# Moving an overflow branch from the front of a mixture-of-experts loop to its end

## The chip, the cores and the metric

The kernel runs on one core of one Trainium2 chip. The metric is the device time of one execution in microseconds (us). The engines that the text names are TensorE (PE, with its weight loads PEld), VectorE (DVE), ScalarE (ACT), GpSimd (POOL) and SyncE (SP), which issues most DMAs. Each engine has its own queue of instructions and goes through it in order. Semaphores make one engine wait for another.

## What is computed

Two layers over 512 positions of width 1024. In each layer a token mixer and a cross-attention to 256 memory positions are projected, added and normalised. Then comes a mixture of 16 experts with two experts for each position:

```python
def grouped_moe(x, router_w, router_b, w_gate, w_up, w_down):
    ...
    combine = jnp.einsum('tk,tke->te', gate,
                         jax.nn.one_hot(idx, N_EXPERTS, dtype=jnp.float32)).astype(x.dtype)
    out = jnp.zeros_like(xt)
    for e in range(N_EXPERTS):
        h = jax.nn.silu(xt @ w_gate[e]) * (xt @ w_up[e])
        out = out + combine[:, e:e + 1] * (h @ w_down[e])
    return out.reshape(bsz, seq, d)
...
    f = grouped_moe(x, router_w, router_b, w_gate[i], w_up[i], w_down[i])
    x = layer_norm(ALPHA * x + f, ln2_g[i], ln2_b[i])
```

The kernel computes each expert for the positions that chose it, up to 128 of them. If an expert was chosen by more, the rest are its overflow. With these inputs no expert overflows.

## The kernel before

*Products.* Every float32 operand is split into a high and a low part, and `mm3` (line 200) makes one product of three matmuls: high by high, high by low and low by high. ACT makes the high part (line 168 for weights, line 207 for activations), DVE the low one (lines 169 and 208).

*Pages and weights.* SBUF is dealt out as 24 pages of equal size, `page` and `drop`, first freed first used. The stream `W` fetches the weights, 1 MB each, by SP (line 147) into a free page, and `pump` fetches and splits as far as pages allow: it leaves `W.keep` pages free, has at most `W.flight` loads in flight and goes down to `W.stop` loads that wait. In the experts the split parts go to a ring of pages of their own (`W.rings(8)`).

*Routing.* `mixer_end` (line 1042) writes the normalised rows to DRAM, into `x1d` (what the experts read) and into `rd` (to which they add), makes the router's tables, and `overflow` (line 599) counts the positions of each expert: `nover` is the number of overflowing blocks, written by DVE at line 610 in the last of four small operations behind the matmuls of line 603.

*Experts.* `experts` (line 651) runs once per layer. POOL gathers the rows of an expert from `x1d` (line 668), PE transposes them (line 677), ACT and DVE split them into `xgt`. Gate and up products follow (`gate_up`, tiles ga and ua), then silu and product h (lines 696, 693), transposes of h (line 702), the down product (tile ya), and POOL scatters the result with addition into `rd` (line 664). The loop is a software pipeline: the down product of expert e-1 comes behind the gate and up products of expert e. PE, ACT and DVE are in an order written by hand (`manual_schedule`) for experts 0 to 14; expert 15 and all else are placed by a scheduler, which may queue an instruction earlier than the text has it when its operands are there. `tc.issue_after(ins)` ties instructions behind `ins` on its engine.

*The branch.* `more` (line 891) reads `nover` into a register of every engine (line 893) and branches (line 894). Behind the branch stands a loop over 48 possible blocks, of which nothing runs here. Its body uses `x1d`, `rd`, `y1` and, before the change, two halves of the page `hy`. In the version before it stands ahead of the first expert's transposes. In the first layer `fill` computes keys and values of the next layer (tile va) just ahead of it; in the second, `fill` does nothing and eight filler matmuls (`keep_warm`, line 299, operands of ones) stand there instead.

*The end of a layer.* For the last expert the scatter is replaced: rows of `rd` are loaded as x (SP, line 768), the layer norm's rows by POOL (line 293), and matmuls add x and the last expert's result (lines 785 to 787). The work for that is again in an order by hand and begins with eight filler matmuls that are tied behind the last up product, `up`.

Of the kernel before, what the change touches and what calls it, by code (L numbers as in the profile page):

```python
# [27 lines left out]
P = 128  # L28
D = 1024
KB = D // P  # L30
# [7 lines left out]
FE = 512  # L38
# [9 lines left out]
def trunk(ctx, tc, x, mem, w_in_a, sgu_ln_g, sgu_ln_b, sgu_w, sgu_b, w_in_b, conv_w, w_kv, w_out,  # L48
# [15 lines left out]
    def page(name, shape, dtype=FT, of=None):  # L64
        of = free_pages if of is None else of
        assert of, f"no page for {name}; held: {sorted(v[1] for v in held.values())}"
        i = of.pop(0)
        uid[0] += 1
        t = pages.tile(shape, dtype, name=f"{name}_{uid[0]}", tag=f"pg{i}", bufs=1)
        held[id(t)] = (i, name, t)  # L70
        return t

    def drop(*ts):
        for t in ts:
            i, name, _ = held.pop(id(t))
            W.home(name).append(i)

    def acc(name="acc"):
        return psum.tile([P, 512], FT, name=name, tag="A", bufs=4)

    def bank(shape, name="bank"):
        return psum.tile(shape, FT, name=name, tag="B", bufs=3)
# [115 lines left out]
    W = Stream()  # L198

    def mm3(o, a, b, start, stop):  # L200

        pe.matmul(o, a[0], b[0], start=start, stop=False)  # L202
        pe.matmul(o, a[0], b[1], start=False, stop=False)  # L203
        return pe.matmul(o, a[1], b[0], start=False, stop=stop)  # L204

    def split_to(hi, lo, src):
        r = act.activation(hi, src, AF.Copy)  # L207
        vec.tensor_tensor(lo, src, hi, op=OP.subtract)  # L208
        return r
# [85 lines left out]
    def keep_warm(n):  # L295

        t = bank([P, 4, P], "warm")
        for _ in range(n):
            pe.matmul(t, ones_b, ones_b[:, None, :].to_broadcast([P, 4, P]), start=True, stop=True)
# [12 lines left out]
    memh = page("memh", [P, KB, NMEM], FR)  # L312
    meml = page("meml", [P, KB, NMEM], FR)
# [5 lines left out]
    def keys_values(after=None):  # L319
        kt = page("kt", [P, 2, H, NMEM], FR)  # L320
        vt = page("vt", [P, 2, 2, MW], FR)
        a = [acc("ka") for _ in range(H)]
        for j in range(4):
            g = W.next()
            for kk in range(2):
                k = 2 * j + kk
                for h in range(H):
                    cs = slice(h * P, (h + 1) * P)
                    mm3(a[h][:, :NMEM], (g[:, 0, kk, cs], g[:, 1, kk, cs]), (memh[:, k, :], meml[:, k, :]),
                        k == 0, k == KB - 1)  # L330
            W.done(g)
        for h in range(H):
            split_to(kt[:, 0, h, :], kt[:, 1, h, :], a[h][:, :NMEM])
        a = [acc("va") for _ in range(2)]
        for j in range(4):
            g = W.next()
            for kk in range(2):
                k = 2 * j + kk
                for m in range(2):
                    ms = slice(m * P, (m + 1) * P)  # L340
                    with ExitStack() if after is None or j < 3 else tc.issue_after(after):
                        mm3(a[m], (memh[:, k, ms], meml[:, k, ms]), (g[:, 0, kk, :], g[:, 1, kk, :]),
                            k == 0, k == KB - 1)
            W.done(g)
        for m in range(2):
            split_to(vt[:, 0, m, :], vt[:, 1, m, :], a[m])
        return kt, vt

    def x_transposed():
        xh = [page("xh", [P, 4, S], FR) for _ in range(2)]  # L350
# [300 lines left out]
    def experts(i, lnp, fill, after, stop, fine=False):  # L651
# [4 lines left out]
        hy = page("h", [P, 4, FE])  # L656
# [15 lines left out]
        def xtrans(e):  # L672
            for q in range(2):
                t = bank([P, 4, P], "xt")
                for k in range(4):
                    k0 = 4 * P * q + 2 * P * (k // 2) + k % 2
                    pe.transpose(t[:, k, :], xg[:, e % 2, k0:k0 + 2 * P - 1:2], ident)  # L677
                split_to(xt[:, 0, 4 * q:4 * q + 4, :], xt[:, 1, 4 * q:4 * q + 4, :], t)
# [38 lines left out]
        def scaled(e):  # L717
            return lambda n, o: act.activation(ys[e % 2][:, n * 512:(n + 1) * 512], o, AF.Copy, scale=tabs[e][1])  # L718
# [3 lines left out]
        if i:  # L722
            with tc.issue_after(last_entry[-1]):
                keep_warm(8)
        fill()
        more(i, hy)
        W.keep, W.flight = 0, 4
        W.ahead, W.whole, W.on_pool = 6, True, lambda n: False
        W.rings(8)
        xtrans(0)  # L730
        gather(2)
        W.pump()
        order = ExitStack()
# [1 line left out]
        for e in range(E):  # L735
            if e == last:
                order.close()
            up = gate_up(e, (lambda: (down(last - 1, scaled(last - 1)), scatter(last - 1))) if e == last else None)
            if e + 1 < E:
                xtrans(e + 1)  # L740
            if e + 3 < E:
                gather(e + 3)
            if e == 5:
                W.parts += 2
            if 0 < e < last:
                down(e - 1, scaled(e - 1))
                scatter(e - 1)
            if e == last - 3:
                W.keep = 4
                W.stop = stop - 2 if stop else 0  # L750
            if e == last:
                W.rings(0)
                drop(xt, xg)
                selp = page("selt", [P, 2, NC, P], FT)
                for c in range(NC):
                    vec.tensor_scalar(selp[:, 0, c, :], slot1, posp[:, c, last:last + 1], None, op0=OP.is_equal)
                t = bank([P, NC, P], "selt")
                for c in range(NC):
                    pe.transpose(t[:, c, :], selp[:, 0, c, :], ident)
                selt = page("selr", [P, NC, P], FR)  # L760
                vec.tensor_copy(selt, t)
                drop(selp)
                xs[:] = [page("x", [P, 2, D]) for _ in range(2)]
                xrow[:] = [xs[c // 2][:, c % 2, :] for c in range(NC)]
                with tc.issue_after(added[last - 1].ins):
                    lnp = ln_params(*lnp, pool_e)
                for c in range(NC):
                    W.behind = sp.dma_start(xrow[c], rd[i][c * P:(c + 1) * P, :]).ins
            if e < last:
                htrans(e)  # L770
# [60 lines left out]
        def half_moments(c):  # L831
            part(c, 0)
            part(c, 1)
            moments(c)

        with tc.manual_schedule(engines={ET.PE, ET.Activation, ET.DVE, ET.Pool}):
            with tc.issue_after(up.ins):
                keep_warm(8)
            htrans(last)
            keep_warm(4)  # L840
            down(last, parts)
            act.activation(lnp[:, 0], lnp[:, 0], AF.Copy, scale=ALPHA)
            if fine:
                for c in range(3):
                    total(c)
                half_moments(0)
                part(1, 0)
                finish(0, "pool")
                after(0)
                part(1, 1)  # L850
                total(3)
                moments(1)
                centred(1)
                finish(1, "both")
                after(1)
                half_moments(2)
                centred(2)
                finish(2, "split")
                after(2)
                half_moments(3)  # L860
                centred(3)
                finish(3, "vec")
                after(3)
            else:
                total(0)
                total(1)
                half_moments(0)
                centred(0)
                finish(0, "dve")
                total(2)  # L870
                half_moments(1)
                centred(1)
                finish(1, "dve")
                after(0)
                total(3)
                W.after = after(1).ins
                half_moments(2)
                if "both" != "pool":
                    centred(2)
                finish(2, "both")  # L880
                half_moments(3)
                if "split" != "pool":
                    centred(3)
                finish(3, "split")
# [95 lines left out]
    W.after = last_mem.ins  # L980
    W.pump()
    W.after = None
    kt, vt = keys_values()
    xh, xl = x_transposed()
    for c in range(NC):
        transposed(xrow[c], KB, lambda q: xh[q], lambda q: xl[q], c * P)
# [16 lines left out]
    a = project_t(xh, xl)  # L1003
# [6 lines left out]
    a = project(xh, xl)  # L1010
# [5 lines left out]
    a = project_t(xh, xl)  # L1016
# [52 lines left out]
    kv1 = []  # L1069
# [4 lines left out]
    def fill0():  # L1074
        W.on_pool = lambda n: False
        kv1.append(keys_values(last_entry[-1]))
        drop(memh, meml)
    xhl = []

    def next_x(c):  # L1080
# [2 lines left out]
        xh, xl = xhl[0]  # L1083
        return transposed(xrow[c], KB, lambda q: xh[q], lambda q: xl[q], c * P)
    experts(0, (ln2_g[0], ln2_b[0]), fill0, next_x, stop)
    kt, vt = kv1[0]
    xh, xl = xhl[0]


# [1 line left out]
    a = project_halves(xh, xl)  # L1091
# [7 lines left out]
    a = project_t(xh, xl)  # L1099
    for h in range(H):  # L1100
        act.activation(cgp[:, h, :], a[h], AF.Copy)
    a = project_t(xh, xl)
# [7 lines left out]
    a = project_t(xh, xl)  # L1110
# [48 lines left out]
```

## Time and profile before

| | us |
|---|---|
| median of 3 timed runs | 1035.75 |
| lowest and highest of them | 1032.32, 1035.86 |
| the profiled execution | 1031.97 |
| its span, first to last instruction | 1030.1 |

The profile is of one execution. Of each instruction it has start and duration, of each idle stretch of an engine what ended it, of each window the granted TensorE clock (1.00 is 2.4 GHz, 0.50 is 1.2 GHz). The experts of the first layer run from about 213 to 510 us, those of the second from about 706 to 1007 us. "Idle before" in a timeline is the wait of the engine just ahead of a row, with what ended it.

### The profile page before, as it was taken

What the parts mean: (1) busy time and instruction counts of PE and PEld (TensorE: products, weight loads), DVE (VectorE), ACT (ScalarE), POOL (GpSimd) and SP (SyncE); (2) the same over time, 40 slices, a digit from 0 to 9 for tenths busy, and PEclk for the clock granted to TensorE, in tenths of its full rate; (3) what the DMA queues carried; (4) which work ended last, traced back from release to release, by engine and by line L of the source; (5) the groups of instructions that cost most, each with busy time, mean ns of one, the idle gap of its engine ahead of it and who ended that gap; (6) DMA issues with size and microseconds to landing.
All of it is one profiled execution on the core that took longest, in us unless ns stands there. A gap on an engine that the chain in (4) does not pass through costs nothing. (4 is left out here: it accounts for less than half of the span.)

```text
span 1030.1 us, 12721 instructions
## 1 busy us (share of the span) xinstructions
PE 983.7 (95%) x4815; PEld 810.6 (79%) x4816; DVE 774.2 (75%) x884; ACT 627.7 (61%) x684; POOL 200.5 (19%) x111
## 2 busy tenths in 40 slices
PE   8999999969999999999999999977899999999995
PEld 6788888858888888888679887865688888888873
DVE  4738567867989898898894455675689898988975
ACT  4626532556788787878643414233687887878763
POOL 0000002112332413321110000221133324233023
PEclk9999999989999999999999999987899999999998
DMA  9813266667999999999880425490799999999944
GB/s 321 294 42 123 91 237 247 244 225 265 364 367 333 366 360 360 360 357 362 282 320 1 164 82 207 131 396 25 232 330 362 372 327 383 359 362 355 357 87 160
DMA packets 102219, 273.30 MB, mean 265 GB/s; under 512 B 10442, under 2 KB 10966, under 8 KB 102152
## 3 DMA queue, kind: packets, MB, share of 16 engines
q1 hardware_dynamic: 89480, 242.84, 64.5%
q0 software_dynamic: 11808, 26.97, 9.4%
q10 hardware_dynamic: 864, 2.62, 0.7%
q8 instruction: 39, 0.64, 0.2%
q14 instruction: 28, 0.23, 0.1%
HBM read 262.22 MB, written 26.21 MB: 280 GB/s over the span
## 5 line engine op out<-in xcount | busy, mean ns | idle before, releaser
L169 DVE TENSOR_TENSOR low<-raw,high 128x2048 fp32r<-128x2048 f32 x189 | 427.9, 2288 | 80.9 <-ACT high L168 79.4
L168 ACT ACTIVATE high<-raw 128x2048 fp32r<-128x2048 f32 x189 | 355.1, 1910 | 22.7 <-PE ga L204 10.1
L668 POOL DMA_INDIRECT xg<-x1d,idxs x32 | 83.2, 2601 | 299.6 <-PE xt L677 270.5
L168 ACT ACTIVATE split<-raw 128x1024 fp32r<-128x1024 f32 x66 | 68.9, 1058 | 71.1 <-PE za L204 26.0
L202 PE MATMUL ya<-high,ht 128*128 128x512 f32 x256 | 103.8, 406 | 0.0
L169 DVE TENSOR_TENSOR split<-raw,split 128x1024 fp32r<-128x1024 f32 x61 | 73.6, 1221 | 39.6 <-ACT split L168 38.9
L204 PE MATMUL ga<-high,xgt 128*128 128x512 f32 x248 | 99.1, 399 | 2.9 <-DVE xgt L208 2.9
L204 PE MATMUL ya<-high,ht 128*128 128x512 f32 x256 | 101.3, 396 | 0.1
L203 PE MATMUL ya<-low,ht 128*128 128x512 f32 x256 | 101.1, 395 | 0.0
L202 PE MATMUL ga<-high,xgt 128*128 128x512 f32 x248 | 100.7, 406 | 0.1
L203 PE MATMUL ga<-low,xgt 128*128 128x512 f32 x248 | 98.4, 397 | 0.0
L204 PE MATMUL ua<-high,xgt 128*128 128x512 f32 x248 | 97.1, 392 | 0.0
L202 PE MATMUL ua<-high,xgt 128*128 128x512 f32 x248 | 96.9, 391 | 0.0
L203 PE MATMUL ua<-low,xgt 128*128 128x512 f32 x248 | 96.8, 390 | 0.0
L169 POOL TENSOR_TENSOR split<-raw,split 128x1024 fp32r<-128x1024 f32 x5 | 11.9, 2383 | 267.0 <-DVE sto L475 147.0
L202 PE MATMUL za<-xh,split 128*128 128x512 f32 x160 | 61.6, 391 | 2.0 <-ACT xh L207 2.0
L203 PE MATMUL za<-xl,split 128*128 128x512 f32 x160 | 62.5, 391 | 0.0
L204 PE MATMUL za<-xh,split 128*128 128x512 f32 x160 | 61.5, 389 | 0.0
L204 PEld LDWEIGHTS ga<-high,xgt 128*128 128x128 f32 x248 | 47.4, 191 | 14.1 <-DVE xgt L208 4.0
L204 PEld LDWEIGHTS ya<-high,ht 128*128 128x128 f32 x256 | 48.1, 188 | 12.8 <-DVE ht L208 1.3
L664 POOL DMA_INDIRECT rd<-h,idxs x16 | 40.4, 2523 | 89.3 <-ACT h L718 79.6
L202 PEld LDWEIGHTS ya<-high,ht 128*128 128x128 f32 x256 | 48.4, 189 | 10.5 <-ACT ht L207 0.6
(250 smaller groups left out, 1886.2 us busy)
## 6 DMA issues: line engine op xcount, KB each, us to landing
raw<-in_w_gate_dram SPq DMA_DIRECT2D x64, 1024.0 KB, 9.8
raw<-in_w_up_dram SPq DMA_DIRECT2D x64, 1024.0 KB, 9.6
raw<-in_w_down_dram SPq DMA_DIRECT2D x64, 1024.0 KB, 10.5
raw<-in_w_kv_dram SPq DMA_DIRECT2D x8, 1024.0 KB, 7.4
raw<-in_w_out_dram SPq DMA_DIRECT2D x8, 1024.0 KB, 8.0
raw<-in_w_in_b_dram SPq DMA_DIRECT2D x8, 1024.0 KB, 11.1
raw<-in_w_in_a_dram SPq DMA_DIRECT2D x6, 1024.0 KB, 5.4
x1d<-x POOLq DMA_DIRECT2D x8, 512.0 KB, 6.0
```

What stands on the lines that cost most here:

```text
L168: act.activation(high, src, AF.Copy)
L169: (pool_e if self.on_pool(self.count) else vec).tensor_tensor(low, src, high, op=OP.subtract)
L202: pe.matmul(o, a[0], b[0], start=start, stop=False)
L203: pe.matmul(o, a[0], b[1], start=False, stop=False)
L204: return pe.matmul(o, a[1], b[0], start=False, stop=stop)
L664: added[e] = pool_e.indirect_dma_start(out=rd[i], out_offset=bass.IndirectOffsetOnAxis(ap=tabs[e][0], axis=0), in_=ys[e % 2], in_offset=No ...
L668: pool_e.indirect_dma_start(out=xg[:, e % 2], out_offset=None, in_=x1d[i], in_offset=bass.IndirectOffsetOnAxis(ap=tabs[e][0], axis=0), bou ...
```

## The change

The call of `more` goes from ahead of the first expert's transposes to the last expert, behind its gate and up products, the down product and scatter of expert 14 and the transposes of the last selection matrix. It gets a page of its own (`rest`) instead of `hy`, for which one page more is kept free from expert 12 on (`W.keep = 5`). In the first layer the transposes of expert 0 are now tied behind the last matmul of `fill`, which `keys_values` returns for that. At the end the first eight filler matmuls are no longer tied behind `up`.

```diff
--- before.py
+++ after.py
@@ -339,12 +339,12 @@
                 for m in range(2):
                     ms = slice(m * P, (m + 1) * P)
                     with ExitStack() if after is None or j < 3 else tc.issue_after(after):
-                        mm3(a[m], (memh[:, k, ms], meml[:, k, ms]), (g[:, 0, kk, :], g[:, 1, kk, :]),
-                            k == 0, k == KB - 1)
+                        end = mm3(a[m], (memh[:, k, ms], meml[:, k, ms]), (g[:, 0, kk, :], g[:, 1, kk, :]),
+                                  k == 0, k == KB - 1)
             W.done(g)
         for m in range(2):
             split_to(vt[:, 0, m, :], vt[:, 1, m, :], a[m])
-        return kt, vt
+        return kt, vt, end.ins
 
     def x_transposed():
         xh = [page("xh", [P, 4, S], FR) for _ in range(2)]
@@ -722,12 +722,12 @@
         if i:
             with tc.issue_after(last_entry[-1]):
                 keep_warm(8)
-        fill()
-        more(i, hy)
+        end = fill()
         W.keep, W.flight = 0, 4
         W.ahead, W.whole, W.on_pool = 6, True, lambda n: False
         W.rings(8)
-        xtrans(0)
+        with ExitStack() if i else tc.issue_after(end):
+            xtrans(0)
         gather(2)
         W.pump()
         order = ExitStack()
@@ -746,7 +746,7 @@
                 down(e - 1, scaled(e - 1))
                 scatter(e - 1)
             if e == last - 3:
-                W.keep = 4
+                W.keep = 5
                 W.stop = stop - 2 if stop else 0
             if e == last:
                 W.rings(0)
@@ -760,6 +760,9 @@
                 selt = page("selr", [P, NC, P], FR)
                 vec.tensor_copy(selt, t)
                 drop(selp)
+                rest = page("more", [P, 4, FE])
+                more(i, rest)
+                drop(rest)
                 xs[:] = [page("x", [P, 2, D]) for _ in range(2)]
                 xrow[:] = [xs[c // 2][:, c % 2, :] for c in range(NC)]
                 with tc.issue_after(added[last - 1].ins):
@@ -834,8 +837,7 @@
             moments(c)
 
         with tc.manual_schedule(engines={ET.PE, ET.Activation, ET.DVE, ET.Pool}):
-            with tc.issue_after(up.ins):
-                keep_warm(8)
+            keep_warm(8)
             htrans(last)
             keep_warm(4)
             down(last, parts)
@@ -980,7 +982,7 @@
     W.after = last_mem.ins
     W.pump()
     W.after = None
-    kt, vt = keys_values()
+    kt, vt, _ = keys_values()
     xh, xl = x_transposed()
     for c in range(NC):
         transposed(xrow[c], KB, lambda q: xh[q], lambda q: xl[q], c * P)
@@ -1075,6 +1077,7 @@
         W.on_pool = lambda n: False
         kv1.append(keys_values(last_entry[-1]))
         drop(memh, meml)
+        return kv1[0][2]
     xhl = []
 
     def next_x(c):
@@ -1083,7 +1086,7 @@
         xh, xl = xhl[0]
         return transposed(xrow[c], KB, lambda q: xh[q], lambda q: xl[q], c * P)
     experts(0, (ln2_g[0], ln2_b[0]), fill0, next_x, stop)
-    kt, vt = kv1[0]
+    kt, vt, _ = kv1[0]
     xh, xl = xhl[0]
```

## Rows read from the trace of the kernel before

**Rows 1.** Page, part 1: busy us (share of the span) xinstructions
```profile
PE 983.7 (95%) x4815; PEld 810.6 (79%) x4816; DVE 774.2 (75%) x884; ACT 627.7 (61%) x684; POOL 200.5 (19%) x111
```

**Rows 2.** Windows, inside the second layer's loop: stretch, length, busy per engine, clock, DMA
```profile
759.64:777.57 17.93, 17.93 (x86) 14.87 (x85) 15.79 (x11) 14.37 (x13) 5.66 (x2) 1.00 0.99 357
```

**Rows 3.** Timeline of PE, first layer's front: start, us, what, [idle before, releaser]
```profile
213.43 1.95 PE L677 MATMUL xt<-ident,xg 128*128 128x128 f32 x8 [7.40 <-DVEq L894]
...
216.24 0.63 PE L204 MATMUL ga<-split,xgt 128*128 128x512 f32 x1
```

**Rows 4.** Lines 893 and 894, first layer's front: ns min/median/max, first and last start
```profile
L893 PEldq TENSOR_LOAD <-nover x1: 487/487/487, 211.9 to 211.9; - x1
...
L894 SPq EVENT_SEMAPHORE  x9: 17/17/17, 218.8 to 220.1; - x9
...
L894 PEldq COMPARE_BRANCH  x1: 353/353/353, 212.5 to 212.5; - x1
```

**Rows 5.** Timeline of DVE, first layer's front
```profile
205.80 4.50 DVE L169 TENSOR_TENSOR low<-raw,high 128x2048 fp32r<-128x2048 f32 x2 [2.38 <-ACT high L168]
...
211.73 0.14 DVE L610 CAST nover<-ovn 1x1 int32<-1x1 f32 x1
...
215.20 0.69 DVE L208 TENSOR_TENSOR xgt<-xt,xgt 128x512 fp32r<-128x512 f32 x1 [3.33 <-ACT xgt L207]
```

**Rows 6.** Timeline of POOL: first gather of the first and of the second layer
```profile
204.17 1.08 POOL L668 DMA_INDIRECT xg<-x1d,idxs  x1 [22.48 <-DVE gates L635]
...
701.36 1.08 POOL L668 DMA_INDIRECT xg<-x1d,idxs  x1 [6.09 <-DVE gates L635]
```

**Rows 7.** Tile xg at both fronts: gathers from issue to landing, us
```profile
DMA to landing us min/median/max: 4.2/5.2/6.2
...
DMA to landing us min/median/max: 3.7/4.3/4.3
```

**Rows 8.** Windows, first layer's front: columns as in rows 2
```profile
211.00:213.00 2.00, 0.00 (x0) 0.00 (x0) 0.88 (x4) 0.06 (x1) 0.00 (x0) 0.50 0.78 280
...
217.50:227.50 10.00, 10.00 (x45) 8.28 (x44) 4.59 (x2) 6.42 (x5) 0.00 (x0) 0.99 0.48 172
...
229.00:231.50 2.50, 0.81 (x3) 0.30 (x2) 2.50 (x3) 2.50 (x4) 2.50 (x1) 0.98 0.10 38
...
231.50:234.50 3.00, 2.91 (x7) 2.33 (x8) 3.00 (x4) 0.36 (x1) 0.29 (x1) 0.50 0.85 255
```

**Rows 9.** Windows, second layer's front: columns as in rows 2
```profile
706.00:709.00 3.00, 2.98 (x11) 2.53 (x12) 1.05 (x2) 1.87 (x3) 0.75 (x1) 0.50 0.03 11
```

**Rows 10.** Timeline of PE, second layer's front
```profile
706.02 1.95 PE L677 MATMUL xt<-ident,xg 128*128 128x128 f32 x8 [2.12 <-PEq L894]
```

**Rows 11.** Timelines of PE and DVE, end of the second layer's loop
```profile
998.04 1.90 PE L299 MATMUL warm<-ones_b 128*128 128x512 bf16 x8
...
999.78 0.60 PE L702 MATMUL htr<-ident,h 128*128 128x128 f32 x4
...
998.31 0.69 DVE L693 TENSOR_TENSOR h<-h,ua 128x512 f32<-128x512 f32 x1 [0.69 <-PE ua L204]
```

**Rows 12.** End of the first layer's loop: timeline of SP, then a wait (us, times, longest)
```profile
485.66 2.92 SPq L147 DMA_DIRECT2D raw<-in_w_in_b_dram  x2
...
503.63 2.47 SPq L768 DMA_DIRECT2D x<-rd  x4
...
PEld ra L785 <- DMA x<-rd: 0.5, 1, 0.5
```

**Rows 13.** Page, part 6: DMA issues, KB each, us to landing
```profile
raw<-in_w_in_b_dram SPq DMA_DIRECT2D x8, 1024.0 KB, 11.1
```

**Rows 14.** Layer norm rows, first layer's end: POOL, landing, first use on ACT
```profile
498.32 1.22 POOL L293 DMA_DIRECT2D ln<-in_ln_g_dram  x1
...
DMA to landing us min/median/max: 8.7/9.1/9.4
...
511.21 1.05 ACT L842 ACTIVATE ln<-ln 128x1024 f32<-128x1024 f32 x1
```

## Prediction

> **What bounds the kernel now.** I read the busy shares first: PE is busy for 95% of the span [rows 1]. Next I read the windows of one expert's length inside the loop: 17.93 us of PE work in 17.93 us, at full clock [rows 2]. So TensorE is the bound of the loops, and a gain can only come from PE's idle or slow stretches at the ends of the loops. The chain of waits names nothing ahead of 705 us, so for the first layer I went to the timelines around the two places that the branch leaves and the two that it goes to. The reader is to see in them when each engine reaches the branch and what PE does meanwhile.
>
> **The front of the first layer.** PE stands idle for 7.40 us and begins the transposes of the first expert (line 677) at 213.43, released by the branch [rows 3]. The branch waits for `nover`, and this waits on DVE: its queue holds two splits of weights, the eviction of the values and the overflow counts, and `nover` is written at 211.73 + 0.14 = 211.87 [rows 5]. From there PE needs 213.43 - 211.87 = 1.56 us: the register load is 0.49, the compare 0.35, the rest is the skipped path's semaphores and the restart [rows 4]. The change takes the wait out. What is late next has two candidates.
> The gather of expert 0 is issued at 204.17 [rows 6] and lands 4.2 to 6.2 us later [rows 7], so the transposes could start at 208.4 to 210.4. After that DVE's low half of the transposed rows binds: the third matmul of each triple needs it, and the first such matmul (line 204) runs at 216.24 [rows 3], behind the low half at 215.20 to 215.89 [rows 5]. DVE is taken until 211.87. If the new low half queues behind all of that, it ends at 211.87 + 0.69 = 212.6; if it goes ahead of the values and counts, at 210.3 + 0.7 = 211.0. The gain is therefore 216.24 - 212.6 = 3.6 us at least and 216.24 - 211.0 = 5.2 at most. I take 4.0, near the lower end, because the values' and the counts' operands are there first.
> The clock adds to it. It fell to its lower level (1.2 GHz, 0.50) in the idle time and PE worked at it from 213.43 until about 217.7 [rows 8]: 4.3 us in which half was lost, 2.1 us. A shorter gap may leave the clock up (2.1 gained) or not (0). A later row says that a short gap is no guarantee: after a wait of 1.7 us in 229 to 231.5 the next 3 us ran at 0.50 [rows 8]. I take 1.0. First layer's front: 4.0 + 1.0 = 5.0 us, between 3.6 and 7.3.
> SP's queue was held too, until its nine semaphore steps ended at 220.1 [rows 4], since the skipped path waits until the loads in flight have landed. I cost that at nothing: the next load waits for a page that DVE frees, and this moves with PE.
>
> **The front of the second layer.** Here PE waits 2.12 us for the branch and starts at 706.02 [rows 10]. The gather is issued at 701.36 [rows 6] and lands after 3.7 to 4.3 us [rows 7], at 705.1 to 705.7. So 0.4 to 1.0 us are free, at the lower clock [rows 9], where a us is worth half: 0.2 to 0.5. I take 0.4.
>
> **The ends.** The branch comes behind the last up product, and PE has no hole there: eight filler matmuls run from 998.04 directly behind the products, then the transposes of h at 999.78, while DVE delivers h at 998.31 + 0.69 = 999.0 [rows 11]. The register load needs only `nover`, long known, and where the branch isn't taken no engine waits for another there: at the old place PE went on at 213.43 while SP was held until 220.1 [rows 3, 4]. The price is each engine's own passage. Queued behind it on PE are the fillers, the transposes and the last down product, and ACT, DVE and everything to the end wait for those. From above the price is the 1.56 us of [rows 3, 5]; from below it is 0, if the fillers go ahead of the branch into an earlier gap (998.04 + 1.56 is then 999.6, and the transposes started at 999.78 anyway). I take 1.2, nearer to the upper end, since the fillers lose the order that tied them to the up product but stay ahead of the transposes. ACT's and DVE's passages lie beside PE's. In the second layer the whole 1.2 counts. In the first, PE then waits 0.5 us for the first row block of x [rows 12], and this slack takes some: 0.7. Together 1.9 us, between 0 and 3.1.
> PE's compare alone takes 0.35 us [rows 4]. The Trainium skill (Runtime: NRT & Kernel Launch, Instruction fetch mechanics) says that a taken branch whose target lies outside the code already fetched has to wait for a fetch. By that rule this part is paid again at the new place; were it free there, the sum below would be 0.7 us better.
> Other steps of the move. The loads of x (SP, line 768) read `rd` and queue behind SP's branch, which waits for the loads in flight. In the first layer these are two of the next projection, issued at 485.66 in 2.92 us [rows 12] and 11.1 us under way [rows 13], so landed by 499.7; the x loads go at 503.63 [rows 12], when the last scatter lands. Cover: 3.9 us. In the second layer nothing is in flight. POOL passes the branch between the last scatter and the layer norm's rows (line 293, at 498.32 [rows 14]), at most 1.6 us; these rows also get a page that is freed about 2 us later, since `rest` takes the one before. Landing 8.7 us after issue [rows 14], they come at about 509 instead of 507, and ACT first uses them at 511.21 [rows 14]: hidden, with 2 us to spare. The ring of raw pages is as large as before, because with keep 5 one page more merely lies ready for `rest`: nothing.
>
> **Sum.** -5.0 - 0.4 + 1.9 = -3.5 us. The profiled execution took 1031.97 us (span 1030.1 and 1.9 around it), which would become 1028.5. The three timed runs went from 1032.32 to 1035.86 with a median of 1035.75, 3.8 above the profiled one. On the scale of the median the sum gives 1032.3.
>
> **Rivals.**
> *All of the front comes back* (0.22): the low half goes early, the clock stays up, the second slow stretch at 231.5 to 234.5 [rows 8], which cost half of 3 us, goes too, and the ends hide in the wait for h: -5.2 - 2.1 - 1.5 - 0.5 + 0.7 = -8.6, so 1027.1. For it: each part is seen in a row. Against it: all have to come together.
> *The ends eat the front* (0.13), the other side: PE's passage leaves a hole ahead of the fillers at both ends, and the clock falls behind it, as behind the 1.7 us hole of [rows 8]. Price for each layer: 1.56 and half of 3 us, 3.1; both 6.2. With the front at its lower end, -3.6 - 0.2, that is +2.4: 1038.1. It decides from the point where both ends cost over 2.7 us each, against the front's 5.4. For it: the filler matmuls stand behind the branch. Against it: PE is busy at both ends up to the branch and the hole is shorter than 1.7.
> *SP's branch delays x* (0.03): more loads in flight than the two. SP was held from 212.4 to 220.1 at the old place [rows 4], 7.7 us; less the cover of 3.9 and with the sum it gives +0.3, 1036.1.
> *The change doesn't do what it says* (0.02): the branch is queued early again. Its body writes `rd`, which the last scatter adds to, so it can't pass this. Time as before, 1035.75.
>
> **How the numbers follow.** The forecast has 0.60; its own range is -1 to -6, 1029.8 to 1034.8. About 0.5% is what a measurement of this kernel can tell from no change: 5.2 us, and the forecast lies within. The range takes in the first rival with its 1027.1 and the second with its 1038.1: 1026.5 to 1038.5. Faster by over 0.5%: the first rival and a little of the forecast's tail, 0.25. Slower by over 0.5%: the far end of the second and third, 0.05. Same: 0.70.
>
> **What would show it.** In the profile after: the wait of line 677 for line 894 gone in both layers; first transposes at about 208.5 to 210.5, first line 204 matmul of expert 0 at 211 to 212.6; the loop at 17.93 us as before; lines 893 and 894 at the layer's end, with 1 to 1.6 us between PE's last up product and what follows; x loads still released by the last scatter. The prediction is wrong if DVE's order at the front keeps the low half behind more than the values, if the clock falls at an end, or if PE meets the branch in the midst of products that were dense before.

## The result, and the profile after

| | before | after |
|---|---|---|
| median of 9 runs each, same chip, us | 1033.41 | 1037.32 |
| lowest, highest | 1029.68, 1035.86 | 1036.58, 1038.56 |
| profiled execution, and its span | 1031.97, 1030.1 | 1036.76, 1035.1 |

The ratio after to before is 1.0051, with a 95% interval of 1.0035 to 1.0067: the change makes the kernel about 5 us slower. The forecast was 3.5 us faster. The two profiled spans differ by 5.0 us too, so the timelines can account for the loss. I did that by taking the same instruction at the borders of each stretch in both traces:

| instruction on PE (gather: POOL) | before | after | difference | stretch behind it |
|---|---|---|---|---|
| first transposes of expert 0, first layer | 213.43 | 208.38 | -5.05 | |
| last up product, first layer | 500.21 | 495.68 | -4.53 | front: -4.5 |
| first ra matmul, first layer | 509.68 | 512.47 | +2.79 | end: +7.3 |
| first gather, second layer | 701.36 | 705.96 | +4.60 | mixer between: +1.8 |
| last up product, second layer | 997.81 | 1000.91 | +3.10 | front: -1.5 |
| first ra matmul, second layer | 1007.10 | 1012.04 | +4.94 | end: +1.8 |

At the front PE's wait for the branch is gone, as forecast, against [rows 3]. Timeline of PE, first layer's front, after the change (start, us, what, [idle before, releaser]):

```profile
208.38 1.24 PE L677 MATMUL xt<-ident,xg 128*128 128x128 f32 x8 [2.25 <-DMA xg<-x1d,idxs]
...
212.35 0.79 PE L204 MATMUL ga<-split,xgt 128*128 128x512 f32 x1 [1.34 <-DVE xgt L208]
```

The transposes now wait for the gather, and the third matmul of the first triple waits for DVE's low half. These are the two candidates that the prediction named as late next.

The loss is at the first layer's end. Its timeline on PE, against [rows 11] (which are of the second layer; the first looks alike, with the transposes of h 1.97 us behind the start of the last up product in both):

```profile
495.68 0.39 PE L204 MATMUL ua<-high,xgt 128*128 128x512 f32 x1
501.38 3.59 PE L299 MATMUL warm<-ones_b 128*128 128x512 bf16 x8 [5.31 <-DVEq L896]
504.76 1.06 PE L702 MATMUL htr<-ident,h 128*128 128x128 f32 x4
```

The reader is to see three things. PE stands still for 5.31 us behind its last up product. What releases it is not PE's own branch but DVE's (the branch is now line 896). And the eight fillers, 1.90 us before, take 3.59. The clock tells why (windows: stretch, length, busy per engine, granted clock, DMA):

```profile
501.30:505.00 3.70, 3.62 (x10) 1.48 (x11) 0.00 (x0) 0.00 (x0) 0.00 (x0) 0.50 0.98 341
```

The granted clock is 0.50, the level of 1.2 GHz, after an idle stretch of 5.3 us. Now DVE over the same time, and the branch's own instructions on PE and DVE (ns min/median/max, first and last start), against [rows 4]:

```profile
496.17 0.69 DVE L693 TENSOR_TENSOR h<-h,ua 128x512 f32<-128x512 f32 x1 [0.46 <-PEq L896]
496.77 4.49 DVE L169 TENSOR_TENSOR low<-raw,high 128x2048 fp32r<-128x2048 f32 x2
```

```profile
L896 PEldq EVENT_SEMAPHORE  x2: 51/51/51, 496.1 to 496.3; - x2
...
L896 DVEq EVENT_SEMAPHORE  x2: 21/21/21, 501.3 to 501.4; - x2
...
L896 PEldq COMPARE_BRANCH  x1: 228/228/228, 493.6 to 493.6; - x1
...
L896 DVEq COMPARE_BRANCH  x1: 72/72/72, 498.2 to 498.2; - x1
```

PE's sequencer compares at 493.6, while its products still run, and is past the skipped path at 496.3: PE's own passage is nearly free. DVE compares at 498.2 but passes only at 501.3, which is when its two splits of weights, queued behind h and ahead of the branch, end (496.77 + 4.49 = 501.26). PE's first filler starts at 501.38.

The second layer has one operation less in that place. DVE and PE there:

```profile
1001.40 0.69 DVE L693 TENSOR_TENSOR h<-h,ua 128x512 f32<-128x512 f32 x1 [0.71 <-PEq L896]
1003.27 2.29 DVE L169 TENSOR_TENSOR low<-raw,high 128x2048 fp32r<-128x2048 f32 x1 [1.18 <-DVEq L896]
```

```profile
1003.05 1.90 PE L299 MATMUL warm<-ones_b 128*128 128x512 bf16 x8 [1.76 <-DVEq L896]
```

DVE's own passage there (ns, first and last start):

```profile
L896 DVEq EVENT_SEMAPHORE  x2: 21/21/21, 1003.0 to 1003.1; - x2
...
L896 DVEq COMPARE_BRANCH  x1: 56/56/56, 1002.4 to 1002.4; - x1
```

No split stands between h and the branch, DVE passes at 1003.0, and PE's hole is 1.76 us; the fillers behind it take 1.90 us again. Of this hole 0.8 us go until h is done (1001.40 + 0.69 = 1002.09, PE's products end at 1001.30). The other 0.96 us are DVE's own load, compare and passage; in the first layer the load and the compare ran beside the splits.

In the list of waits the two holes are one line (us, times, longest):

```profile
PE warm L299 <- DVEq L896: 7.1, 2, 5.3
```

Why a filler that reads only ones should wait for DVE can be read in the code, and the experiments test the reading. `bank` is a ring of three PSUM banks. The branch's body takes it three times for its transposes (tile mxt), which the body's DVE reads; the next to take a bank of that ring is the fillers' tile. So the first filler carries a wait for DVE's count behind the body. Where the body is skipped, DVE adds these counts on its way past, once its own queued work is done.

### The profile page after: what moved, and what is told of

The parts are those of the page before. It is cut to its first block, busy times and chain, and to the rows that moved or that the text cites. A ratio compares the mean times of both kernels' runs of the same rounds, so it can differ in the third digit from the quotient of the medians.

```text
span 1035.1 us, 12717 instructions
## 1 busy us (share of the span) xinstructions
PE 984.0 (95%) x4815; PEld 810.2 (78%) x4816; DVE 774.0 (75%) x884; ACT 625.5 (60%) x682; POOL 200.6 (19%) x111
## 5 line engine op out<-in xcount | busy, mean ns | idle before, releaser
L204 PEld LDWEIGHTS ya<-high,ht 128*128 128x128 f32 x256 | 48.1, 188 | 12.5 <-DVE ht L208 0.9
L207 ACT ACTIVATE xgt<-xt 128x512 fp32r<-128x512 f32 x64 | 34.9, 596 | 36.8 <-PE xt L677 36.7
```

## Experiments

Theory A: the ends cost what they do because PE waits, through a shared bank (A1), for DVE's passage, which lasts until DVE's own queue is empty (A2). Rival B: a taken branch has a fixed price on each engine. A theory C came up on the way. Ratios are to the kernel before on the same chip. Spans of different chips differ (the same place ahead of any change lies up to 2 us apart), so stretches are compared within a trace: from the start of the last up product to the transposes of h, and to the first ra matmul. Before, these are 1.97 and 9.5 us (first layer), 1.97 and 9.3 (second); after the change 9.08 and 16.8, 3.88 and 11.1.

### No branch at the end

```diff
-                more(i, rest)
```

> The changed kernel with the branch itself left out (both layers; the overflow path is not computed), all other parts of the change kept: the tied transposes, keep 5, the page, the untied fillers. Theory A (all of the loss is the passage of the branch at the two ends): the holes ahead of the first fillers (5.31 us in the first layer, 1.76 in the second) go, the first ra matmul comes about 7.3 us earlier in the first layer, the second end gives 1.9 back; 1035.1 - 7.3 - 1.9 = 1025.9 us of span, within 1.5. Rival (other parts of the change cost it: keep 5 or untied fillers): the span stays at 1030 or more.

Ratio 0.9987 (0.9972 to 1.0002), span 1030.8. From the last up product to ra: 9.3 and 9.6 us, so both holes are gone. Yet the span is not the 1025.9 us expected, and the whole is not clear of the kernel before. The rival of this run, another part of the change, was right as well; the timeline of PE shows which:

```profile
486.69 0.27 PE L759 MATMUL selt<-ident,selt 128*128 128x128 f32 x1
486.80 1.89 PE L299 MATMUL warm<-ones_b 128*128 128x512 bf16 x8
488.53 0.49 PE L759 MATMUL selt<-ident,selt 128*128 128x128 f32 x3
```

With the tie gone and no branch to hold them, the fillers run 13 us earlier, amid products that were dense.

### The body's transposes on a bank of their own

```diff
-                        t = bank([P, 4, P], "mxt")
+                        t = psum.tile([P, 4, P], FT, name="mxt", tag="R", bufs=1)
```

> The changed kernel with one edit in the branch's body: its transposes (tile mxt) go to the PSUM bank of the small tables and no longer to the ring of three that the fillers and the transposes of h use. Theory A1 (PE's first filler waits for DVE to pass its branch, because it takes the bank that the body's DVE reads; DVE passes late): fillers run directly behind the last up product, no hole over 0.7 us there; first layer's end 6 to 7 us better; in the second layer DVE still passes between h and the low half of ht, 0.5 to 1.5 us of its 1.9 stay; span 1027 to 1029. Rival B (each engine pays a fixed price of 1.8 to 5 us for a taken branch, a fetch of code, wherever it stands): PE's holes stay, wherever the branch comes to lie, span 1033 or more.

Tag R is the bank of the small tables. Ratio 1.0049 (1.0031 to 1.0068), span 1033.8. The total is B's, the trace is not. No filler and no transpose of h waits for the branch: the transposes of h stand 1.24 us behind the last up product in both layers. The time went to two other places. The fillers ran early, as in the run before (at 486.04). And the branch, now behind the transposes of h, holds the last down product:

```profile
500.14 0.66 PE L702 MATMUL htr<-ident,h 128*128 128x128 f32 x4 [0.85 <-DVE h L693]
500.63 1.03 PE L299 MATMUL warm<-ones_b 128*128 128x512 bf16 x4
503.32 0.50 PE L202 MATMUL ya<-high,ht 128*128 128x512 f32 x1 [1.67 <-ACTq L896]
```

That product's bank is one of the four of `acc`, of which the body's ACT reads some; now the branch of ACT is named as the releaser. That looks like the same mechanism on another bank and engine; no run tests it by giving this product a bank of its own. I had expected 1027 to 1029 because I counted neither the fillers nor this wait.

### The splits held until behind the branch

```diff
-             up = gate_up(e, (lambda: (down(last - 1, scaled(last - 1)), scatter(last - 1))) if e == last else None)
+             up = gate_up(e, (lambda: (down(last - 1, scaled(last - 1)), scatter(last - 1), setattr(W, 'hold', True))) if e == last else None)
...
                  drop(rest)
+                 W.hold = False
```

> The changed kernel, but the stream of weights is held from expert 14's scatter until behind the branch, so that DVE's two splits of 2.25 us no longer stand between h and its branch in the first layer; the bank is shared as in the changed kernel. Theory A2 (DVE's skipped path waits until its own queued work is done, and PE waits for that): the first layer's hole falls from 5.31 to 1.5 to 2.0 us, as in the second layer, and the fillers stay at or come back sooner to full clock; first layer's end 4 to 5.5 us better, span 1030 to 1031.5, unless the later splits hold the last down product or the next projection. Rival B (fixed price, or a fetch that queues behind the weights' loads): hole stays near 5, span 1034 to 1036.

Ratio 1.0000 (0.9983 to 1.0016): the 5 us that the change lost against the kernel before are back. PE and DVE at the first layer's end:

```profile
498.27 0.69 DVE L693 TENSOR_TENSOR h<-h,ua 128x512 f32<-128x512 f32 x1 [0.29 <-PEq L897]
502.62 0.69 DVE L208 TENSOR_TENSOR ht<-htr,ht 128x512 fp32r<-128x512 f32 x1 [3.67 <-ACT ht L207]
```

```profile
499.62 1.90 PE L299 MATMUL warm<-ones_b 128*128 128x512 bf16 x8 [1.46 <-DVEq L897]
```

The hole is 1.46 instead of 5.31 us, and the fillers are at full clock. The second layer, which had no splits to hold, stays at 1.76. B's fixed price would have left both.

### More work for DVE in the second layer

```diff
...
+                if i:
+                    with tc.issue_after(made[0]):
+                        vec.memset(rest, 0.0)
                 more(i, rest)
```

(`made[0]` is h's instruction; the lines that keep it are left out.)

> The changed kernel with more work for DVE ahead of its branch in the second layer alone: a memset of the branch's page tied behind h, and with it one split of 2.29 us comes to lie ahead of the branch, as two do in the first layer. Theory A2 (the hole lasts until DVE's own queue is done): the second layer's hole grows from 1.76 by the split and the memset less what the register load hid, to 4 to 5.5 us; the first layer's stays at 5.3; span 3 to 5 us above the changed kernel's, ratio to the kernel before 1.008 to 1.010. Rival B (fixed price of the taken branch): hole stays at 1.8, ratio 1.005.

Ratio 1.0113 (1.0092 to 1.0133). The opposite test, and the second layer now looks like the first:

```profile
1003.47 1.76 DVE L766 MEMSET more<- 128x2048 f32 x1 [0.38 <-issue]
1005.15 2.23 DVE L169 TENSOR_TENSOR low<-raw,high 128x2048 fp32r<-128x2048 f32 x1
```

```profile
1007.49 3.59 PE L299 MATMUL warm<-ones_b 128*128 128x512 bf16 x8 [5.20 <-DVEq L899]
```

The hole ends 0.11 us behind DVE's last operation (1005.15 + 2.23 = 1007.38). Behind the hole of 5.20 us the clock falls here too: the fillers take 3.59 us and no longer 1.90. I had not counted that, and the ratio lies above the 1.008 to 1.010 expected. A2 holds in both directions.

### Fillers ahead of the branch

```diff
+                with tc.issue_after(up.ins):
+                    keep_warm(8)
                 rest = page("more", [P, 4, FE])
...
-            keep_warm(8)
             htrans(last)
```

> The changed kernel with the first eight fillers put ahead of the branch, tied behind the last up product as before the change. Theory A1: they fill the start of the hole instead of coming behind it; the hole moves to between the fillers and the transposes of h, about 3.5 us in the first layer and 0 to 0.5 in the second; transposes of h at about 501.4 instead of 504.76 and 1003.1 instead of 1004.8; span 1030 to 1032. Rival (the fillers cost nothing where they are): span unchanged at 1034 to 1036.

Ratio 1.0034 (1.0017 to 1.0051). From the last up product to the transposes of h: 5.79 us instead of 9.08, and 2.58 instead of 3.88, about as expected. At the first ra matmul only half of that is left: 15.2 us instead of 16.8, and 10.5 instead of 11.1. In the first layer the clock stays at 0.50 into the last down product (503 to 508 us), and in the second PE then waits 0.68 us for the low half of ht. So the span, 1035.9 us, misses the 1030 to 1032 expected, and moving the fillers wins only half of what the transposes show. In the first layer the transposes of h take the next bank of the ring and wait for DVE in the fillers' place:

```profile
503.60 1.09 PE L702 MATMUL htr<-ident,h 128*128 128x128 f32 x4 [3.66 <-DVEq L897]
```

### Both of these

The edits of the held splits and of the fillers ahead of the branch together.

> The held splits and the fillers ahead of the branch together, bank shared. Theories A1 and A2 together: from the last up product to the transposes of h 3.2 us become 2.0 to 2.4 in the first layer and 3.5 become 2.0 in the second; span 1032.5 - 1.0 - 1.5 = 1030, ratio 0.9975. Rival (fixed price of the taken branch that PE pays behind the fillers as well): 3.2 and 3.5 stay, ratio 1.000.

Ratio 0.9972 (0.9956 to 0.9989), faster than both kernels. The first layer's end:

```profile
493.95 1.90 PE L299 MATMUL warm<-ones_b 128*128 128x512 bf16 x8
496.30 0.63 PE L702 MATMUL htr<-ident,h 128*128 128x128 f32 x4 [0.45 <-PEq L898]
```

The second layer has the same 0.45 us. Here PE's own branch is the releaser, and this is its price: 0.45 us of idle time, where the prediction took 1.2 (the transposes of h stand 2.58 us behind the last up product, 0.6 later than before). By B it would have been 1.8 to 5 us.

### No branch, fillers tied; own bank, fillers tied

```diff
-            keep_warm(8)
+            with tc.issue_after(up.ins):
+                keep_warm(8)
             htrans(last)
```

in the kernel without a branch and in the one with a bank of its own.

> As the run without a branch (overflow path left out), but the first eight fillers tied behind the last up product again, as before the change. There the untied fillers ran in the midst of expert 15's products (486.80, 1.89 us), in both layers. Theory C (a second part of the change costs: with nothing that holds them, untied fillers go into dense products and cost their 1.9 us each time): 1030.8 - 3.8 = 1027.0 of span, ratio to the kernel before 0.995 (0.993 to 0.997). This is also what the front alone gives. Rival (PE would have waited for h at the end anyway, so that the fillers' place is free): ratio stays at 0.998 to 0.999.

> As the run with the body's transposes on a bank of their own, with the first fillers tied behind the last up product again. Theory C: the fillers' 1.9 us come back in both layers, span 1033.8 - 3.6 = 1030.2, ratio 1.001. What stays is the branch between the fillers and the last down product: in the first layer the down product waits for ACT's passage (1.67 us in the run before), since its bank is one that the body's ACT reads; in the second DVE's passage ahead of the low half of ht (1.56 us). Rival (the fillers' place is free): ratio 1.004 to 1.006.

Without a branch: 0.9942 (0.9919 to 0.9964), against 0.9987 untied. With a bank of its own: 0.9988 (0.9972 to 1.0003), against 1.0049 untied, a little better than the 1.001 expected. In the latter the transposes of h are back at 1.97 us in both layers, as in the kernel before, though the branch is there; the last down product still waits 1.67 us for ACT's branch in the first layer and, in the second, 0.89 us for DVE's low half of ht.

### One part of the change alone: fillers untied

```diff
-            with tc.issue_after(up.ins):
-                keep_warm(8)
+            keep_warm(8)
```

in the kernel before.

> One part of the change alone: the kernel before, branch at the front, with its first eight fillers at the end no longer tied behind the last up product. Theory C: they go into expert 15's products in both layers and cost 1.9 us each, less about 0.4 that the transposes of h come sooner behind the products: ratio 1.002 to 1.004. Rival (free, as the prediction had it): 1.000.

Ratio 1.0038 (1.0022 to 1.0054). PE has them amid expert 15 in both layers:

```profile
490.69 1.89 PE L299 MATMUL warm<-ones_b 128*128 128x512 bf16 x8
...
986.64 1.89 PE L299 MATMUL warm<-ones_b 128*128 128x512 bf16 x8
```

C holds. In the changed kernel itself this price is not seen, because there the bank holds the fillers behind the branch.

### The branch at the front, with a bank of its own

The edit of the bank, in the kernel before.

> The kernel before with one edit: the body's transposes on the bank of the small tables; branch and counts stay at the front. Theory A1 (the 7.40 us at the front, too, were PE's wait through the shared bank): the first expert's transposes go when the gather has landed, 208.4 to 210.5, and not at 213.43; the branch then stands between them and the first product, which still waits for the late count: first product at about 214.2 instead of 215.2, ratio 0.998 to 1.000. Rival (the transposes waited for the branch because it stands ahead of them in the text, whatever the bank): transposes at 213.4 as before, ratio 1.000.

Ratio 1.0011 (0.9999 to 1.0023).

```profile
208.50 1.20 PE L677 MATMUL xt<-ident,xg 128*128 128x128 f32 x8 [2.27 <-DMA xg<-x1d,idxs]
214.57 0.77 PE L202 MATMUL ga<-split,xgt 128*128 128x512 f32 x1 [4.88 <-PEq L894]
```

The transposes go at 208.50 and not at 213.43, with the branch still at the front: the wait of 7.40 us in [rows 3] was the shared bank's too, and what releases them is the gather. No time is won, since the first product now stands behind the branch, which still waits for the late `nover`.

### The branch at the front, with an early count

```diff
...
-                    with ExitStack() if after is None or j < 3 else tc.issue_after(after):
+                    tie = after and (counted[0] if kk else after)
+                    with ExitStack() if after is None or j < 3 else tc.issue_after(tie):
...
+        counted[:] = [m.ins]
...
```

The bank's edit, and the last six matmuls of the values tied behind the counting matmuls (`counted[0]`).

> The kernel before, with the branch left at the front: its body's transposes on the bank of the small tables, and the counting matmuls moved ahead of the last six matmuls of the values, so that the overflow count is written before DVE's splits. Theory A (the 7.40 us at the front were PE's wait, through the shared bank, for DVE's passage behind the late count): the first expert's transposes go at 208.4 to 210.5, the gain of the front (4.5 us) is there and the ends are as before; ratio 0.995 to 0.996, span about 1027.5. Rival B (fixed price of a taken branch): PE meets the branch between the transposes and the first product and stands there 2 to 5 us: ratio 0.998 to 1.001.

Ratio 0.9970 (0.9956 to 0.9984), faster than both kernels though the branch is not moved, and less than the 0.995 to 0.996 expected: here too the clock fell at the front (0.50 from 214.2 to 218.2). The overflow is known before DVE's splits. PE stands 0.83 us at the branch, released by ACT's, two products ahead of one that waits 1.07 us for DVE's low half anyway:

```profile
212.22 0.79 PE L202 MATMUL ga<-split,xgt 128*128 128x512 f32 x1 [0.83 <-ACTq L898]
```

## Why the prediction was wrong

*The front of the first layer: the size by luck.* Forecast -5.0, measured -4.5. The step of DVE's low half held: it queued behind the values, and the first line 204 matmul came 3.9 us sooner (4.0 taken). The clock's term did not. PE, transposes of experts 1 and 2, before and after:

```profile
227.41 1.11 PE L677 MATMUL xt<-ident,xg 128*128 128x128 f32 x8
...
243.68 1.11 PE L677 MATMUL xt<-ident,xg 128*128 128x128 f32 x8
```

```profile
224.74 1.11 PE L677 MATMUL xt<-ident,xg 128*128 128x128 f32 x8
...
239.13 1.11 PE L677 MATMUL xt<-ident,xg 128*128 128x128 f32 x8
```

At expert 1 only 2.7 of the 3.9 us are left, because the clock fell here too and PE worked longer at the lower level behind that matmul. From the first line 204 matmul to these transposes it took 11.2 us before and 12.4 after; in the three traces of the experiments in which the clock stayed up it took 10.6. So the term was a loss of 1.2 here and a gain of 0.6 at best, where a gain of 1.0 out of 0 to 2.1 was taken: a part of the old slow stretch lies ahead of that matmul and is in the 4.0 already. At expert 2 the lead is 4.6 us, because the second slow stretch of [rows 8] is gone (granted clock 1.00 from 229.5 to 232.5). In all nine traces with the change, with or without its branch, these two groups of transposes lie 14.4 us apart, in the two kernels with the old front 16.2 and 16.3. The forecast had left that stretch to its first rival. The two errors cancel.

*The front of the second layer: right, and luck beside it.* Forecast -0.4; the transposes bring 0.34 (gather +4.60, transposes +4.26). The measured -1.5 comes from further on: between the transposes of experts 1 and 2 the same matmuls take 19.8 us instead of 21.0, since fewer of them run at the lower clock. That isn't the move. The traces of the experiments show either 19.7 to 19.9 or 20.9 to 21.2 us there, and three of the four with the branch at the front are among the short ones.

*The ends: this step failed.* It says that "where the branch isn't taken no engine waits for another there", on the evidence that PE went on while SP was held. That shows it for SP alone. [rows 3] named the engine that PE did wait for: the releaser of the 7.40 us was DVE's branch. I read that row as PE's own passage. At the old place the two can't be told apart: all engines waited for the same `nover`, and in the trace of before PE is past the skipped path at 213.1 and DVE at 213.2. From this came two wrong terms. "ACT's and DVE's passages lie beside PE's": at the first end DVE's ends 5.0 us after PE's (501.3 against 496.3). And the price of 0 to 1.56, with 1.2 taken, which is the price of neither: PE's own is 0.45 us, what it waits for is 1.76 and 5.31. Measured 7.3 and 1.8 us, together 9.2, against 1.9. Of the 7.3 some 5.3 are the hole and 1.6 the eight fillers at the lower clock (501.38 to 504.76, against 500.44 to 502.18 before).

*The rival "the ends eat the front"* had the sign, the fall of the clock (seen at the first end alone) and nearly the time (1038.1), at 0.13. Its mechanism was another, a hole of PE's own. It argued against itself that the hole is shorter than 1.7 us.

*Costed at nothing, and so it was:* SP's queue and the loads of x (they go at 499.09, 4.5 us sooner than before), the layer norm's rows. *Costed at nothing and wrong by itself:* the tie of the fillers; the move hides it.

*Not in the sum:* the mixer between the layers takes 1.8 us longer. Most of it arises at one place, where DVE normalises the last row blocks. DVE there, before and after (line 811 has become 814):

```profile
528.36 1.18 DVE L169 TENSOR_TENSOR split<-raw,split 128x1024 fp32r<-128x1024 f32 x1
...
529.51 1.41 DVE L811 SCALAR_TENSOR_TENSOR x<-x,mv,ln 128x512 f32<-128x512 f32 x2
```

```profile
531.30 2.31 DVE L169 TENSOR_TENSOR split<-raw,split 128x1024 fp32r<-128x1024 f32 x2
...
533.58 1.40 DVE L814 SCALAR_TENSOR_TENSOR x<-x,mv,ln 128x512 f32<-128x512 f32 x2
```

After the change one more split of weights stands ahead of the normalisation, and PE's transposes of x come some 1.2 us later behind the first ra matmul. All nine traces with the move's other edits have four splits there, also those without a branch, and the router's logits come 165.3 to 165.6 us behind the first ra matmul. All four traces with the branch at the front have three, and 164.2 to 164.3, also the one with the early count, which starts its experts sooner. So it goes with another edit of the change, perhaps the page more that is kept free or the pages' new order; which one, and the rest of the 1.8, stay open. `W.keep`, costed at nothing, is thus not cleared.

The rule of the Trainium skill that the prediction cited (Runtime: NRT & Kernel Launch, Instruction fetch mechanics) has a taken branch wait for a fetch when its target lies outside the code at hand. By the runs, whatever of that shows on PE lies within its 0.45 us of idle time. On DVE some 0.5 us lie between the end of the compare (1002.4 + 0.06) and the passage (1003.0) at the second end with nothing else queued, and no run shows what they are. Neither is the 5.31 us of the first end. PE's compare itself took 0.23 and 0.34 us at the new place, while its products still ran.

## What to carry to other kernels

A branch that is never taken still takes part in the order of buffers: whoever next takes a bank or page that its body uses waits for each engine that uses it there, and each engine gets past only when its own queue is done. That is shown here for PSUM banks; no run tests a page. Before moving a branch, list these buffers and the next to take them, and look what stands queued on the slowest of those engines. Read the releaser that a row names as it stands, also where it is an engine that one did not expect; and a filler without a tie is only as harmless as the thing that happens to hold it.

## What was not expected of the hardware

The clock at the first layer's front fell in some executions and not in others with the same instructions and nearly the same idle time ahead. The windows from 4 us behind the first transposes, of the changed kernel and of the kernel without a branch and with tied fillers:

```profile
212.38:216.38 4.00, 4.00 (x10) 3.18 (x11) 0.79 (x4) 1.91 (x1) 0.00 (x0) 0.52 1.01 388
```

```profile
211.91:215.91 4.00, 3.72 (x16) 3.11 (x17) 1.65 (x6) 1.92 (x1) 0.00 (x0) 1.00 1.02 386
```

PE had stood idle for 2.25 us before the transposes in the one and 1.94 in the other; a third, the run with held splits and fillers ahead of the branch, had 2.30 and full clock. From the first transposes to those of expert 2 the five traces with the move and a clock at 0.50 to 0.52 in this window take 30.8 to 31.2 us, the three at 1.00 take 28.8 to 29.2, and the last, at 0.72, 30.9: some 2 us of span, and no run shows what decides. The 1.0 that the prediction took for the clock fits neither.

A branch's parts are cheap by themselves: the register's load took 0.29 to 1.05 us, the compare 0.05 to 0.36, and PE's sequencer does both while earlier matmuls still run (compare at 493.6, products until 496.07).
